# Two heads at a time in three attention branches: probability-times-value products that alternate between partitions of a PSUM bank

## The chip, the cores and the metric

One core of one Trainium2 chip runs the whole program. The metric is device time in microseconds (us) of one execution, given as the median of several runs. Engines are named as in the profile: PE is TensorE's matmul row, PEld its weight load row, DVE is VectorE, ACT is ScalarE, POOL is GpSimd, SP is SyncE, whose queue issues nearly all DMAs. L634 is line 634 of the kernel.

## The reference, cut to what matters

Two transformer layers over 512 tokens of width 1024. Each has a mixer of four attention branches and then a feed-forward part (dense in layer 0, 8 experts in layer 1). All products keep float32 accuracy. What the change touches is the softmax attention of branches b, c and d:

```python
# b: 4 heads, 96-wide queries and keys, 64-wide values, causal, blocks of 128 queries
s = einsum('bqhd,bkhd->bhqk', qf[:, i*128:L], kf[:, :L]) * scale        # L = 128 * (i + 1)
p = softmax(where(mask, s, -inf), axis=-1)
outs.append(einsum('bhqk,bkhd->bqhd', p, v[:, :L]))
# c: 8 query heads on 2 key heads, 32-wide, a band of two blocks of 128 keys, bias, a sink in the denominator
# d: 3 patterns of 4 heads, 32-wide, bands of strided keys, mixed by their log-sum-exp
```

## The kernel before

**The stage.** In each layer `merge` interleaves generators: `attend`, which runs the units of branches b, d and c in that order, and a filler chain of `front_c` (projections for branch c) and `gates` (gated output products of branches a, b and d, the `mm` matmuls of L208, L210 and L212). The framework's scheduler then orders each engine's instructions when the program is built, by program order and by when it expects operands and buffers to be ready; on the chip each engine runs its list in that fixed order.

**Units.** `attend` (L614) takes units from `branch_b`, `branch_d` and `branch_c`. A unit is part of one head: the scores of one or two blocks of 128 queries (PE into an `sc` bank), `smax` (L596: DVE adds mask or bias, takes the maximum, writes to a `big` tile) and `expo` (L603: ACT). In branch b a head has three units (query blocks 0 and 1 together, block 2, block 3, that is 3, 3 and 4 blocks of 128 keys), in branches c and d two (3 and 4 blocks, in d's second group 4 and 4). That makes 12, 16 and 16 units in a layer: 20 with 3 blocks and 24 with 4.

**Lags.** `step` (L639) keeps three units in the list `ts` and up to three in `vs` (`lt=3`, `lv=3`). For each new unit it first calls `times` for the oldest turned unit, then `turn` for the oldest unit in `ts`. `turn` (L618) transposes the unit's 3 or 4 probability blocks on PE (L622) into a `tr` bank and copies that bank to a `pt` tile, on ACT (L628) and DVE (L626) in turn. `times` (L632) multiplies: for each block one float32 matmul (L634) with the value block, 128x32 (c, d) or 128x64 (b), as the stationary operand and the 128x128 transposed probabilities as the moving one. A float32 matmul shows in the trace as two passes, each a weight load and a matmul record. The output goes to 32 or 64 partitions of one `pv` bank, the partitions of that head: `rs`, or `slice(64 * s_, 64 * s_ + 64)`. The last unit of a bank calls `after`, which scales and evacuates it.

**Heads.** `heads(h)` prepares the operands of one head ahead of its units. In branch b it is two `head_T` calls (L730: 8 transposes, then `split` into `op` tiles, ACT L187 and DVE L188), called for the next head after the third query block's scores. In branches c and d it is `stack`: DMAs on the SP queue (L844) into `op` or, for odd heads, `opx` tiles, and in d a bias table from `toeplitz` (L332); each head calls it for the next one as its first unit begins. Branch c asks for its bias table (`fsw`) as the head begins. `op` has 10 buffers, `opx` 8, `big` 5, `pt` 3, `sc` 2, `tr` 2, `pv` 1, the bias tables `fb` 2.

Of the kernel before, what the change touches and what calls it, by code (L numbers as in the profile page):

```python
# [7 lines left out]
F32 = mybir.dt.float32  # L8
# [29 lines left out]
B_ = dict(mm=3, sc=2, tr=2, pv=1, t2=11, op=10, big=5, u96=2, pt=3, small=24, go=6, raw=4, whi=3, wlo=2, fb=2, gx=4, mraw=4, mhi=5, mlo=5, mg=3, r4=8)  # L38
# [54 lines left out]
def build(tc, A, out, dbg=None):  # L93
# [5 lines left out]
    with es:  # L99
# [249 lines left out]
        def mixer(l, norm, follow, fargs):  # L349
# [264 lines left out]
            def attend(units):  # L614

                def turn(p, perm, blocks, mid, after):  # L618
                    got = mid and mid()
                    ps = trp()  # L620
                    for b, (c, *_) in enumerate(blocks):
                        nc.tensor.transpose(ps[:, 128 * b:128 * b + 128], p[:, c:c + 128], perm)  # L622
                    pt = at.tile([128, 512], F32, tag="pt", name="pt", bufs=B_["pt"])
                    n = 128 * len(blocks)
                    if attend.n % 2:
                        nc.vector.tensor_copy(pt[:, :n], ps[:, :n])  # L626
                    else:
# [20 lines left out]
                for u in units:  # L648
# [5 lines left out]
                    yield  # L654
                while ts or vs:
                    step(True)
                    yield
# [112 lines left out]
            def branch_b(qt, kt, v):  # L770
# [5 lines left out]
                if True:  # L776
                    nxt = heads(0)
                    for h in range(4):
                        t, s_ = divmod(h, 2)
                        if s_ == 0:  # L780
                            pv, nm, li = Bank(), stat(2), stat(2)
                        qh, ql, kh, kl = nxt
                        p = big(1280)
                        c = 0
                        blocks = []
                        for i in range(NB):
                            w = 128 * (i + 1)
                            if i != 1:
                                bank = sc()
                            ps = bank[:, 128:384] if i == 1 else bank[:, :w]  # L790
                            qs = slice(128 * i, 128 * i + 128)
                            scores3(ps, qh[:, qs], ql[:, qs], kh[:, :w], kl[:, :w])
                            smax(ps, causal[:, 512 - w:], p[:, c:c + w], BIG, nm[:, i, s_:s_ + 1])
                            expo(p[:, c:c + w], nm[:, i, s_:s_ + 1], li[:, i, s_:s_ + 1])
                            for kb in range(i + 1):
                                blocks.append((c + 128 * kb, pv, (slice(64 * s_, 64 * s_ + 64), qs),
                                               v[:, kb, 64 * h:64 * h + 64], kb == 0, kb == i))
                            c += w
                            if i == 2 and h < 3:
                                nxt = heads(h + 1)  # L800
                            if i:
# [11 lines left out]
                                yield p, ident, blocks, mid, after  # L813
                                blocks = []
# [50 lines left out]
            def branch_c(kn, q, v):  # L865
# [4 lines left out]
                nxt = heads(0)  # L870
                yield iter(())
                o = []

                if True:
                    for h in range(8):
                        t, s_ = divmod(h, 4)
                        rs = slice(32 * s_, 32 * s_ + 32)
                        if s_ == 0:
                            pv, nm, li = Bank(), stat(4), stat(4)
                            kst = nxt[0]  # L880
                        qst = nxt[1]
# [4 lines left out]
                        p = big(896)  # L886
                        c = 0
                        for i in range(NB):
                            nb = 2 if i else 1
                            w = 128 * nb  # L890
                            k0 = 128 * (i + 1) - w
                            qs = slice(128 * i, 128 * i + 128)
                            if i % 2 == 0:
                                bank = sc()
                                b0 = c
                                blocks = []
                            ps = bank[:, c - b0:c - b0 + w]
                            nc.tensor.matmul(ps, qst[:, qs], kst[:, k0:k0 + w], start=True, stop=True)
                            smax(ps, f[:, 256 - w:], p[:, c:c + w], nsink[:, h:h + 1], nm[:, i, s_:s_ + 1])
                            expo(p[:, c:c + w], nm[:, i, s_:s_ + 1], li[:, i, s_:s_ + 1])  # L900
                            for b in range(nb):
                                blocks.append((c + 128 * b, pv, (rs, qs), v[:, k0 // 128 + b, 32 * t:32 * t + 32],
                                               b == 0, b == nb - 1))
                            c += w
                            if i % 2:
                                mid = after = None
                                if s_ == 3 and i == NB - 1:
                                    nc.vector.tensor_sub(nm, nm, nsink[:, 4 * t:4 * t + 4].unsqueeze(1)
                                                         .to_broadcast([128, NB, 4]))
                                    nc.scalar.activation(nm, nm, AF.Exp)  # L910
                                    nc.vector.tensor_add(li, li, nm)
                                    nc.vector.reciprocal(li, li)

                                    def mid(rb=widen(li)):
                                        return spread(rb, flip)

                                    def after(r, t=t, pv=pv):
                                        o.append(oevac(pv[:], r, t2() if t else None))
                                        if t:
                                            st["oc"] = o  # L920
                                yield p, flip, blocks, mid, after
# [15 lines left out]
            def branch_d(q, k, v):  # L937
# [13 lines left out]
                nxt = heads(0, 0)  # L951
# [51 lines left out]
                for g in range(2):  # L1003
                    for h in range(4):
                        rs = slice(32 * h, 32 * h + 32)
                        qst, kst, f = nxt
# [3 lines left out]
                        c = 0  # L1010
                        for b0 in (0, 2):
                            ps = sc()
                            blocks = []
                            c0 = c
                            cols = []
                            for b in (b0, b0 + 1):
                                bs = slice(128 * b, 128 * b + 128)
                                if g:
                                    w = 256
                                    for j in range(2):  # L1020
                                        nc.tensor.matmul(ps[:, c - c0 + 128 * j:c - c0 + 128 * j + 128],
                                                         qst[j][:, bs], kst[j][:, bs], start=True, stop=True)
                                        blocks.append((c + 128 * j, pv[1], (rs, bs),
                                                       v[:, b, 128 + 128 * j + 32 * h:160 + 128 * j + 32 * h],
                                                       j == 0, j == 1))
                                else:
                                    w = 256 if b else 128
                                    k0 = 128 * b + 128 - w
                                    nc.tensor.matmul(ps[:, c - c0:c - c0 + w], qst[0][:, bs], kst[0][:, k0:k0 + w],
                                                     start=True, stop=True)  # L1030
                                    for j in range(w // 128):
# [863 lines left out]
```

## Time and profile before

| | |
|---|---|
| median of 3 runs | 1424.32 us (1423.17 to 1425.55) |
| the profiled execution | 1422.78 us, span 1420.8 us |
| granted clock over the span | 0.986 |
| PE busy | 1360.3 us, 96% |
| DVE, ACT, POOL busy | 841.8 us, 777.9 us, 383.9 us |

The span is the time from the first to the last instruction of the program. A busy time is the union of an engine's records. Matmuls are pipelined, so their records overlap, and a busy PE is not necessarily one at its peak. The chain that ended last is followed back from the last instruction, at each step to what released it.

### The profile page before, as it was taken

How to read it: one execution, taken by the hardware profiler on the slowest of the kernel's cores; microseconds unless marked ns; L12 is line 12 of the kernel's file. 1: busy time of each engine (PE TensorE's matmuls, PEld its weight loads, DVE VectorE, ACT ScalarE, POOL GpSimd, SP SyncE). 2: the span in 40 equal slices, each digit the busy share in tenths (PEclk: the TensorE clock that was granted, in tenths of full speed). 3: DMA queues.
4: the chain of work that ended last, by engine and by line, in shares of the span. 5: the costliest groups of instructions: out<-in, count | busy, mean ns of one | idle time of the engine just before them, and what ended most of it. 6: DMA issues, size and time to landing. Idle time of an engine off the chain costs nothing.

```text
span 1420.8 us, 21146 instructions
## 1 busy us (share of the span) xinstructions
PE 1360.3 (96%) x7826; PEld 1108.8 (78%) x7826; DVE 841.8 (59%) x1488; ACT 777.9 (55%) x1492; POOL 383.9 (27%) x307
## 2 busy tenths in 40 slices
PE   7999999999999999999999999999998899999996
PEld 5777667877778888888777767787685788989995
DVE  5344656666664444433433655656564879988883
ACT  5255666666453222233234566666544767778884
POOL 2000110023031112101000120002302577877764
PEclk9999999999999999999999999999999899999998
DMA  9422325551373333344432332554453588999994
GB/s 260 111 66 72 105 82 174 156 166 58 93 222 89 95 99 93 108 148 141 116 86 60 95 95 95 184 155 144 137 162 102 196 269 248 305 302 311 315 304 97
DMA packets 241116, 217.15 MB, mean 153 GB/s; under 512 B 12408, under 2 KB 212080, under 8 KB 241008
## 3 DMA queue, kind: packets, MB, share of 16 engines
q1 hardware_dynamic: 237352, 206.25, 47.8%
q0 software_dynamic: 3456, 9.44, 3.1%
q8 instruction: 63, 1.03, 0.3%
q14 instruction: 45, 0.37, 0.1%
q10 hardware_dynamic: 200, 0.06, 0.0%
HBM read 187.32 MB, written 28.38 MB: 152 GB/s over the span
## 4 chain that ended last, share of the span: by engine, by line
PE 74%; issue 10%; ACT 5%; DVE 4%; POOL 4%; DMA 3%; POOLq 0%; SPq 0%; another core or an unknown queue 0%; ACTq 0%; DVEq 0%
PE mm L210 13%; PE mm L212 12%; PE mm L208 11%; PE mg L1586 8%; PE pv L634 5%; PE mg L1589 4%; PE tr L622 3%; PE sc L1119 1%; PE tr L1119 1%; PE pv L576 1%; PE sc L530 1%; POOL mlo L1354 1%; PE tr L822 1%; DVE mlo L1354 1%; PE mg L1434 1%
## 5 line engine op out<-in xcount | busy, mean ns | idle before, releaser
L200 ACT CAST whi<-raw 128x1024 fp32r<-128x1024 f32 (+1 forms) x144 | 141.9, 986 | 190.9 <-PE mm L210 93.6
L1354 DVE TENSOR_TENSOR mlo<-mraw,mhi 128x768 bf16<-128x768 f32 (+2 forms) x160 | 181.3, 1141 | 26.8 <-ACT mhi L1351 25.8
L201 DVE TENSOR_TENSOR wlo<-raw,whi 128x1024 fp32r<-128x1024 f32 (+1 forms) x144 | 165.7, 1153 | 45.4 <-PE mm L212 25.6
L208 PE MATMUL mm<-xh,whi 128*128 128x512 f32 x608 | 162.7, 397 | 2.8 <-ACT xh L190 2.8
L210 PE MATMUL mm<-xl,whi 128*128 128x512 f32 x608 | 155.3, 395 | 0.0
L1351 ACT CAST mhi<-mraw 128x1024 fp32r<-128x1024 f32 (+1 forms) x160 | 151.9, 963 | 4.8 <-DMA mraw<-in_w_down_exp_dram 3.5
L212 PE MATMUL mm<-xh,wlo 128*128 128x512 f32 x608 | 151.1, 390 | 0.0
L1586 PE MATMUL mg<-xcat,mhi 128*128 128x320 f32 x768 | 137.8, 322 | 1.0 <-DVE xcat L188 1.0
L210 PEld LDWEIGHTS mm<-xl,whi 128*128 128x128 f32 x608 | 114.1, 189 | 26.1 <-issue 2.9
L212 PEld LDWEIGHTS mm<-xh,wlo 128*128 128x128 f32 x608 | 114.3, 188 | 24.1 <-issue 0.3
L208 PEld LDWEIGHTS mm<-xh,whi 128*128 128x128 f32 x608 | 110.4, 188 | 23.7 <-ACT xh L190 3.6
L1586 PEld LDWEIGHTS mg<-xcat,mhi 128*128 128x128 f32 x768 | 114.9, 191 | 1.5 <-DVE xcat L188 0.7
L502 POOL TENSOR_TENSOR y<-y,t 128x512 f32<-128x512 f32 x32 | 42.1, 1320 | 258.0 <-DVE t L501 256.4
L1354 POOL TENSOR_TENSOR mlo<-mraw,mhi 128x256 bf16<-128x256 f32 x80 | 97.1, 1216 | 29.9 <-ACT mhi L1351 12.7
L1589 PEld LDWEIGHTS <-mlo 128*128 128x128 bf16 x1152 | 77.3, 99 | 18.0 <-DVE mlo L1354 0.8
L387 DVE TENSOR_TENSOR t<-mm,rb 128x512 f32<-128x512 f32 x41 | 28.3, 691 | 90.9 <-PE mm L212 88.6
L634 PE MATMUL pv<-pt,v 128*32 128x128 f32 (+1 forms) x624 | 81.7, 279 | 0.1
L1586 PE MATMUL mg<-acat,mhi 128*128 128x320 f32 x384 | 75.6, 330 | 2.6 <-POOL acat L1631 2.6
L1184 POOL TENSOR_TENSOR t<-t,t 128x512 f32<-128x512 f32 x16 | 34.2, 2138 | 143.6 <-DVE t L1183 143.6
L247 POOL TENSOR_TENSOR t<-t,t 128x512 f32<-128x512 f32 x21 | 32.8, 1561 | 148.7 <-ACT t L246 148.4
L634 PEld LDWEIGHTS pv<-pt,v 128*32 128x32 f32 (+1 forms) x624 | 60.0, 117 | 15.3 <-issue 9.5
L1589 PE MATMUL mg<-xb,mlo 128*128 128x160 bf16 x768 | 70.5, 235 | 0.4 <-DVE mlo L1354 0.4
(368 smaller groups left out, 2712.5 us busy)
## 6 DMA issues: line engine op xcount, KB each, us to landing
mraw<-in_w_gu_exp_dram SPq DMA_DIRECT2D x48, 1024.0 KB, 7.9
mraw<-in_w_down_exp_dram SPq DMA_DIRECT2D x32, 768.0 KB, 5.3
raw<-in_w_in_dram SPq DMA_DIRECT2D x46, 512.0 KB, 3.9
raw<-in_w_gu_dense_dram SPq DMA_DIRECT2D x32, 512.0 KB, 4.1
heads<-t SPq DMA_DIRECT2D x36, 256.0 KB, 2.0
opx<-heads SPq DMA_DIRECT2D x68, 128.0 KB, 3.4
op<-heads SPq DMA_DIRECT2D x68, 128.0 KB, 3.2
raw<-in_w_down_dense_dram SPq DMA_DIRECT2D x16, 512.0 KB, 4.1
```

What stands on the lines that cost most here:

```text
L200: (nc.gpsimd.tensor_copy if pool else nc.scalar.copy)(hi, raw)
L201: (eng or nc.vector).tensor_sub(lo, raw, hi.bitcast(F32))
L208: nc.tensor.matmul(ps, wh[:, k, :], xs[k][0], start=first and k == 0, stop=False)
L210: nc.tensor.matmul(ps, wh[:, k, :], xs[k][1], start=False, stop=False)
L212: nc.tensor.matmul(ps, wl[:, k, :], xs[k][0], start=False, stop=last and k == n - 1)
L502: (nc.vector if br in YV else nc.gpsimd).tensor_add(y[m], y[m], u)
L622: nc.tensor.transpose(ps[:, 128 * b:128 * b + 128], p[:, c:c + 128], perm)
L634: nc.tensor.matmul(pv[i], lt, pt[:, 128 * b:128 * b + 128], start=st, stop=sp_)
L1351: nc.scalar.copy(self.hi[:, a:b], self.raw[:, a:b])
L1354: eng.tensor_sub(self.lo[:, a:b], self.raw[:, a:b], self.hi[:, a:b].bitcast(F32))
L1586: nc.tensor.matmul(ps[:, j, :2 * CAP], wh[:, k, :], cat[:, k, :], start=k == 0, stop=False, skip_group_check=True)
L1589: nc.tensor.matmul(ps[:, j, :CAP], wl[:, k, :], xb[:, k, :], start=False, stop=k == kk - 1, skip_group_check=True)
```

## The change

`step` takes two turned units at a time and `times` runs their products alternately, block by block. So that the two units of a pair belong to two heads, each branch now makes its units in the order of head pairs: unit 1 of heads h and h+1, then unit 2 of both. Operands of two heads are prepared together: in branch b those of heads 2 and 3 after the last scores of heads 0 and 1, in branches c and d those of the next pair as a pair begins. The bias tables have 4 buffers of 128x256 instead of 2 padded to 128x512. Arithmetic, matmuls and their shapes, lags `lt` and `lv` and the other buffer numbers stay.

```diff
-B_ = dict(..., fb=2, ...)
+B_ = dict(..., fb=4, ...)
...
-                def times(pt, blocks, after, got):
-                    for b, (c, pv, i, lt, st, sp_) in enumerate(blocks):
-                        nc.tensor.matmul(pv[i], lt, pt[:, 128 * b:128 * b + 128], start=st, stop=sp_)
-                    if after:
-                        after(got)
+                def times(*pair):
+                    for b in range(len(pair[0][1])):
+                        for pt, blocks, *_ in pair:
+                            c, pv, i, lt, st, sp_ = blocks[b]
+                            nc.tensor.matmul(pv[i], lt, pt[:, 128 * b:128 * b + 128], start=st, stop=sp_)
+                    for _, _, after, got in pair:
+                        if after:
+                            after(got)
...
-                    if len(vs) >= (1 if last else P_["lv"]):
-                        times(*vs.pop(0))
+                    if len(vs) >= (2 if last else P_["lv"]):
+                        times(vs.pop(0), vs.pop(0))
                     if len(ts) >= (1 if last else P_["lt"] + 1):
                         vs.append(turn(*ts.pop(0)))
...
# branch_b
-                    nxt = heads(0)
-                    for h in range(4):
-                        t, s_ = divmod(h, 2)
...
+                nxt = [heads(0), heads(1)]
+                for t in range(2):
+                    pv, nm, li = Bank(), stat(2), stat(2)
+                    cur, nxt = nxt, []
+                    ps_, banks, c, blocks = [big(1280), big(1280)], [None] * 2, [0, 0], [[], []]
+                    for i in range(NB):
+                        for s_ in range(2):
+                            h = 2 * t + s_
+                            qh, ql, kh, kl = cur[s_]
...
-                            if i == 2 and h < 3:
-                                nxt = heads(h + 1)
+                            if i == NB - 1 and t == 0:
+                                nxt.append(heads(2 + s_))
...
# branch_c
-                    for h in range(8):
...
-                        if h < 7:
-                            nxt = heads(h + 1)
-                        f = at.tile([128, 256], F32, tag="fb", name="fsw", bufs=B_["fb"], padded_shape=[128, 512])
-                        toeplitz(f, h, 256, 256)
+                for hp in range(0, 8, 2):
...
+                    if hp < 6:
+                        nxt = [heads(hp + 2), heads(hp + 3)]
+                    f, p, c = [], [], [0, 0]
+                    for j in range(2):
+                        f.append(at.tile([128, 256], F32, tag="fb", name="fsw", bufs=B_["fb"]))
+                        toeplitz(f[j], hp + j, 256, 256)
+                        p.append(big(896))
+                    for i0 in (0, 2):
+                        for j in range(2):
+                            h, s_ = hp + j, s0 + j
...
# branch_d
-                nxt = heads(0, 0)
+                nxt = [heads(0, 0), heads(0, 1)]
...
-                    for h in range(4):
...
-                        if (g, h) != (1, 3):
-                            nxt = heads(*divmod(4 * g + h + 1, 4))
-                        p = big(1024)
+                    for hp in (0, 2):
+                        cur = nxt
+                        if (g, hp) != (1, 2):
+                            nxt = [heads(*divmod(4 * g + hp + j, 4)) for j in (2, 3)]
+                        p, c = [big(1024), big(1024)], [0, 0]
                         for b0 in (0, 2):
+                            for a_ in range(2):
+                                h = hp + a_
```

## Rows read from the trace of the kernel before

**Rows 1.** The page's first section: busy time of each engine, share, instructions

```profile
PE 1360.3 (96%) x7826; PEld 1108.8 (78%) x7826; DVE 841.8 (59%) x1488; ACT 777.9 (55%) x1492; POOL 383.9 (27%) x307
```

**Rows 2.** Busy time by stretch, all instructions (columns: the second line)

```profile
core 0: us, PE busy (x) PEld busy (x) DVE busy (x) ACT busy (x) POOL busy (x), PEclk, DMA share, GB/s
225.00:352.00 127.00, 123.95 (x798) 98.67 (x798) 81.08 (x240) 80.12 (x223) 20.54 (x16) 1.00 0.48 142
891.00:1019.00 128.00, 125.02 (x788) 99.28 (x788) 80.18 (x239) 79.63 (x222) 19.71 (x16) 0.97 0.50 145
1075.00:1420.00 345.00, 317.63 (x2717) 287.47 (x2715) 269.48 (x388) 245.42 (x414) 235.44 (x194) 0.96 0.82 248
312.00:340.00 28.00, 25.75 (x177) 20.56 (x176) 19.39 (x61) 18.23 (x57) 8.69 (x7) 1.00 0.40 119
...
225.00:245.00 20.00, 19.85 (x118) 15.30 (x118) 14.12 (x33) 15.31 (x34) 0.00 (x0) 1.00 0.69 220
```

**Rows 3.** Busy time by stretch, L634 alone: length, PE (records), PEld, clock, DMA

```profile
225.00:352.00 127.00, 40.44 (x312) 29.79 (x312) 1.00 0.48 142
891.00:1019.00 128.00, 41.30 (x312) 30.25 (x312) 0.97 0.50 145
```

**Rows 4.** PE's timeline in branch c: start, us, engine, line, operation, records

```profile
310.63 0.40 PE L212 MATMUL mm<-goh,wlo 128*128 128x512 f32 x1
310.95 1.06 PE L634 MATMUL pv<-pt,v 128*32 128x128 f32 x8
311.94 0.55 PE L622 MATMUL tr<-c_flip,big 128*128 128x128 f32 x3
...
315.66 0.62 PE L212 MATMUL mm<-goh,wlo 128*128 128x512 f32 x2
...
323.22 0.84 PE L634 MATMUL pv<-pt,v 128*32 128x128 f32 x6
...
324.89 1.31 PE L634 MATMUL pv<-pt,v 128*32 128x128 f32 x14
...
331.21 0.39 PE L898 MATMUL sc<-opx,op 128*128 128x256 f32 x1 [1.39 <-DVE stat L596]
...
338.10 1.96 PE L634 MATMUL pv<-pt,v 128*32 128x128 f32 x20
```

**Rows 5.** The tile view of pv: duration min/median/max ns, first and last start

```profile
L634 PEld LDWEIGHTS pv<-pt,v x624: 106/110/177, 225.9 to 1018.2; 128*32 128x32 f32 x116, 128*64 128x64 f32 x40
L634 PE MATMUL pv<-pt,v x624: 272/273/423, 225.9 to 1018.3; 128*32 128x128 f32 x116, 128*64 128x128 f32 x40
```

**Rows 6.** PE's timeline at four instants: the L634 records then running

```profile
321.94 0.38 PE L634 MATMUL pv<-pt,v 128*32 128x128 f32 x2
...
325.35 0.41 PE L634 MATMUL pv<-pt,v 128*32 128x128 f32 x4
...
338.67 0.49 PE L634 MATMUL pv<-pt,v 128*32 128x128 f32 x3
...
339.22 0.52 PE L634 MATMUL pv<-pt,v 128*32 128x128 f32 x5
```

**Rows 7.** Timelines of ACT, DVE and SP in branch b

```profile
232.05 1.05 ACT L187 CAST op<-tr 96x512 fp32r<-96x512 f32 x2
...
237.28 0.48 ACT L628 COPY pt<-tr 128x384 f32<-128x384 f32 x1
...
233.94 1.28 DVE L188 TENSOR_TENSOR op<-tr,op 96x512 fp32r<-96x512 f32 x2
...
238.93 0.68 DVE L626 COPY pt<-tr 128x512 f32<-128x512 f32 x1
...
233.98 10.14 SPq L844 DMA_DIRECT2D op<-heads  x16
```

**Rows 8.** Waits from 225 to 352 us: total, times, longest

```profile
ACT pt L628 <- PE tr L622: 16.5, 10, 2.6
...
DVE big L596 <- DMA fsw<-relvec: 3.8, 3, 1.7
```

More of the change, by code (lines that the diff above doesn't have):

```diff
@@ L35 @@
 NFT = DFE // 128
-B_ = dict(mm=3, sc=2, tr=2, pv=1, t2=11, op=10, big=5, u96=2, pt=3, small=24, go=6, raw=4, whi=3, wlo=2, fb=2, gx=4, mraw=4, mhi=5, mlo=5, mg=3, r4=8)
+B_ = dict(mm=3, sc=2, tr=2, pv=1, t2=11, op=10, big=5, u96=2, pt=3, small=24, go=6, raw=4, whi=3, wlo=2, fb=4, gx=4, mraw=4, mhi=5, mlo=5, mg=3, r4=8)
 P_ = dict(d=0.0, c=0.0, g=0.0, h=0.0, fb=0.0, fd=0.3, na=54, pa=0, lt=3, lv=3, hg=0, hb=0, ho=0, sa=15, fa=0.125, pb=0, pc=0.4, pd=0.15, eg=0, eb=0)
@@ L654, in attend @@
                     yield
+                assert not len(ts) + len(vs) & 1
                 while ts or vs:
@@ L774, in heads @@
                     return head_T(qt, h) + head_T(kt, h)
-                if True:
-                    nxt = heads(0)
-                    for h in range(4):
-                        t, s_ = divmod(h, 2)
[L780 to L786, printed above, removed]
+                nxt = [heads(0), heads(1)]
@@ L787, in branch_b @@
+                for t in range(2):
[6 more added lines that the diff above has]
+                            qh, ql, kh, kl = cur[s_]
+                            p = ps_[s_]
                             w = 128 * (i + 1)
@@ L798, in branch_b @@
-                            c += w
-                            if i == 2 and h < 3:
-                                nxt = heads(h + 1)
+                                blocks[s_].append((c[s_] + 128 * kb, pv, (slice(64 * s_, 64 * s_ + 64), qs),
+                                                   v[:, kb, 64 * h:64 * h + 64], kb == 0, kb == i))
+                            c[s_] += w
+                            if i == NB - 1 and t == 0:
+                                nxt.append(heads(2 + s_))
@@ L812, in after @@
                                             st["ob"] = o
-                                yield p, ident, blocks, mid, after
-                                blocks = []
+                                yield p, ident, blocks[s_], mid, after
+                                blocks[s_] = []
             def headnorm(t, gain, rev, streams=False):
@@ L868, in heads @@
                     return None if s_ else stack(kn, 32 * t, 1, t % 2), stack(q[t], 32 * s_, 0, s_ % 2)
-                nxt = heads(0)
+                nxt = [heads(0), heads(1)]
                 yield iter(())
                 o = []
-                if True:
-                    for h in range(8):
[L876 to L881, printed above, removed]
-                        if h < 7:
-                            nxt = heads(h + 1)
-                        f = at.tile([128, 256], F32, tag="fb", name="fsw", bufs=B_["fb"], padded_shape=[128, 512])
-                        toeplitz(f, h, 256, 256)
[L886 to L921, printed above, removed]
@@ new lines, in branch_c, with mid, after @@
+                for hp in range(0, 8, 2):
+                    t, s0 = divmod(hp, 4)
+                    if s0 == 0:
+                        pv, nm, li = Bank(), stat(4), stat(4)
+                        kst = nxt[0][0]
+                    cur = nxt
[9 more added lines that the diff above has]
+                            h, s_ = hp + j, s0 + j
+                            rs = slice(32 * s_, 32 * s_ + 32)
+                            bank = sc()
+                            b0 = c[j]
+                            blocks = []
+                            for i in (i0, i0 + 1):
+                                nb = 2 if i else 1
+                                w = 128 * nb
+                                k0 = 128 * (i + 1) - w
+                                qs = slice(128 * i, 128 * i + 128)
+                                ps = bank[:, c[j] - b0:c[j] - b0 + w]
+                                pc = p[j][:, c[j]:c[j] + w]
+                                nc.tensor.matmul(ps, cur[j][1][:, qs], kst[:, k0:k0 + w], start=True, stop=True)
+                                smax(ps, f[j][:, 256 - w:], pc, nsink[:, h:h + 1], nm[:, i, s_:s_ + 1])
+                                expo(pc, nm[:, i, s_:s_ + 1], li[:, i, s_:s_ + 1])
+                                for b in range(nb):
+                                    blocks.append((c[j] + 128 * b, pv, (rs, qs), v[:, k0 // 128 + b, 32 * t:32 * t + 32],
+                                                   b == 0, b == nb - 1))
+                                c[j] += w
+                            mid = after = None
+                            if s_ == 3 and i0:
+                                nc.vector.tensor_sub(nm, nm, nsink[:, 4 * t:4 * t + 4].unsqueeze(1)
+                                                     .to_broadcast([128, NB, 4]))
+                                nc.scalar.activation(nm, nm, AF.Exp)
+                                nc.vector.tensor_add(li, li, nm)
+                                nc.vector.reciprocal(li, li)
+                                def mid(rb=widen(li)):
+                                    return spread(rb, flip)
+                                def after(r, t=t, pv=pv):
+                                    o.append(oevac(pv[:], r, t2() if t else None))
+                                    if t:
+                                        st["oc"] = o
+                            yield p[j], flip, blocks, mid, after
@@ L1003, in branch_d @@
                 for g in range(2):
-                    for h in range(4):
-                        rs = slice(32 * h, 32 * h + 32)
-                        qst, kst, f = nxt
-                        if (g, h) != (1, 3):
-                            nxt = heads(*divmod(4 * g + h + 1, 4))
-                        p = big(1024)
-                        c = 0
-                        for b0 in (0, 2):
[L1012 to L1031, printed above, removed]
-                                        blocks.append((c + 128 * j, pv[0], (rs, bs),
-                                                       v[:, k0 // 128 + j, 32 * h:32 * h + 32],
-                                                       j == 0, j == w // 128 - 1))
-                                cols.append((b, c, w))
-                                c += w
-                            for b, c1, w in cols:
-                                nm = ml[g][:, b, 0, h:h + 1]
-                                smax(ps[:, c1 - c0:c1 - c0 + w], f[:, 256 - w:], p[:, c1:c1 + w], BIG, nm)
-                                expo(p[:, c1:c1 + w], nm, ml[g][:, b, 1, h:h + 1])
-                            yield p, flip, blocks, None, (keep, combine)[g] if (h, b0) == (3, 2) else None
@@ new lines, in branch_d @@
+                    for hp in (0, 2):
+                        cur = nxt
+                        if (g, hp) != (1, 2):
+                            nxt = [heads(*divmod(4 * g + hp + j, 4)) for j in (2, 3)]
+                        p, c = [big(1024), big(1024)], [0, 0]
+                        for b0 in (0, 2):
+                            for a_ in range(2):
+                                h = hp + a_
+                                rs = slice(32 * h, 32 * h + 32)
+                                qst, kst, f = cur[a_]
+                                ps = sc()
+                                blocks = []
+                                c0 = c[a_]
+                                cols = []
+                                for b in (b0, b0 + 1):
+                                    bs = slice(128 * b, 128 * b + 128)
+                                    c1 = c[a_]
+                                    if g:
+                                        w = 256
+                                        for j in range(2):
+                                            nc.tensor.matmul(ps[:, c1 - c0 + 128 * j:c1 - c0 + 128 * j + 128],
+                                                             qst[j][:, bs], kst[j][:, bs], start=True, stop=True)
+                                            blocks.append((c1 + 128 * j, pv[1], (rs, bs),
+                                                           v[:, b, 128 + 128 * j + 32 * h:160 + 128 * j + 32 * h],
+                                                           j == 0, j == 1))
+                                    else:
+                                        w = 256 if b else 128
+                                        k0 = 128 * b + 128 - w
+                                        nc.tensor.matmul(ps[:, c1 - c0:c1 - c0 + w], qst[0][:, bs], kst[0][:, k0:k0 + w],
+                                                         start=True, stop=True)
+                                        for j in range(w // 128):
+                                            blocks.append((c1 + 128 * j, pv[0], (rs, bs),
+                                                           v[:, k0 // 128 + j, 32 * h:32 * h + 32],
+                                                           j == 0, j == w // 128 - 1))
+                                    cols.append((b, c1, w))
+                                    c[a_] += w
+                                for b, c1, w in cols:
+                                    nm = ml[g][:, b, 0, h:h + 1]
+                                    smax(ps[:, c1 - c0:c1 - c0 + w], f[:, 256 - w:], p[a_][:, c1:c1 + w], BIG, nm)
+                                    expo(p[a_][:, c1:c1 + w], nm, ml[g][:, b, 1, h:h + 1])
+                                yield p[a_], flip, blocks, None, (keep, combine)[g] if (h, b0) == (3, 2) else None
```

11 lines of the change are left out of this document (5 added, 6 removed).

## The prediction

> **What bounds the kernel now.** I began with the page's busy times: PE is busy for 96% of the span and DVE and ACT for little over half of theirs [rows 1]. That is an average, so I asked for the two stretches in which the pairs can act, from the first L634 record to the last of each layer: 225 to 352 us and 891 to 1019 us. There PE is busy 123.95 of 127 us and 125.02 of 128 us, DVE about 63%, ACT about 63% [rows 2]. The reader is to see that PE leaves 3 us in each stretch, so that time taken out of PE is time taken out of the kernel until another engine or a wait shows. The products of L634 hold 40.44 and 41.30 us of PE there, 81.74 us in all, a third of the stage [rows 3].
>
> **What one burst costs now.** A unit's `times` is a run of 6 or 8 passes. In PE's timeline 8 passes take 1.06 us and 6 take 0.84 us [rows 4], so a pass adds (1.06 - 0.84) / 2 = 0.11 us, though its record lasts 0.273 us [rows 5]: passes of one head follow each other at 0.11 us, two to three of them in flight (2 at 321.94, 3 at 338.67 [rows 6]).
>
> A burst also costs something at both ends. The 512-column matmuls before one follow each other at 0.62 - 0.39 = 0.23 us, so the one that starts at 310.63 frees the array's input at 310.86; the burst starts at 310.95, 0.09 later. Its last pass starts at 310.95 + 1.06 - 0.27 = 311.74 and the transposes start at 311.94, 0.20 later, 0.09 more than a pass's pace [rows 4]. That is 0.18 us a burst.
>
> **Whether two heads overlap.** The trace of before has a few places where the scheduler put a burst of one head straight behind one of the next head. The run of 14 at 324.89 is 8 passes of one head and 6 of the next, on other partitions. One after the other they would take 1.06 + 6 x 0.11 = 1.72 us; they take 1.31 [rows 4]. In its overlapping part 4 records are in flight, where a single head has 2 or 3 [rows 6]. The run of 20 at 338.10 is the control: it begins with 14 passes of one head, and 0.57 us into it only 3 records are in flight; when the next head's 6 follow, there are 5 [rows 6]. It takes 1.96 us, where 20 passes in a row would take 1.06 + 12 x 0.11 = 2.38 [rows 4]. So the second head rides along, as far as PE's order lets it start early: 0.4 us of its 0.66 us are saved when it stands behind, and with alternating blocks it can start behind the first two passes.
>
> The Trainium skill, in "TensorE: Matmul & The Clock Gate", section "Part 3: Packing small matmuls — row/col tiling", says that weight loads overlap with running matmuls "only when row_grp differs"; all these products use all 128 rows. By that rule every pass of the second head would wait with its load, and pairs would give nothing but fewer bursts (a rival below). The 14 loads of the run above last 0.106 us or more each [rows 5], 1.48 us together, within a run of 1.31 us that has their matmuls in it too, so here the trace does not agree.
>
> **The change part by part.**
>
> *Alternating products.* 88 units become 44 pairs: 20 of 3 blocks a head and 24 of 4. If the second head is hidden but for one half of a pass (between 0, all hidden, and 0.11, a whole pass behind; I take 0.05), a pair takes 0.89 or 1.11 us: 20 x 0.89 + 24 x 1.11 = 44.4 us in place of 81.74 us [rows 3]. That is -37.3 us (bounds -36 and -38.5). The nearest rows, 0.4 us saved in a pair that does not alternate, would give 44 x 0.4 = -17.6 us; I take the alternating value, because the control shows that it is the order alone that delays the second head.
>
> *Fewer bursts.* PE's timeline has 41 runs of L634 in each stretch, 82; there will be 44. 38 x 0.18 = -6.8 us.
>
> So PE loses 44.1 us of work, 22 us in each layer.
>
> *Operands of two heads at a time, branch b.* Of 10 `op` buffers heads 0 and 1 hold 8, so the 8 tiles of heads 2 and 3 can only be written after the last scores of heads 0 and 1, where before the next head was prepared one unit ahead. A head is 4 transposes twice, two casts on ACT (0.525 us each) and two subtractions on DVE (0.64 us each) [rows 7]. Cover: the filler's `mm` products and the six units still in the lags. If that cover is gone, both heads' casts and subtractions lie open, 2 x (1.05 + 1.28) = 4.7 us a layer; below it is 0. I take 1.5 us a layer: +3 us.
>
> *Operands of two heads, branches c and d.* The same DMAs, twice as many at a time, a pair ahead instead of a head ahead, which is the same share of lead and twice as long in time. The SP queue issued 16 of these from 233.98 to 244.12, before any unit of branch d [rows 7], so the fetches run far ahead of use. Behind them on SP stand the gates' weights and bias tables. 0.
>
> *Four bias buffers.* Same bytes. A table of branch c can be fetched while two pairs are in hand, not two heads. DVE waited 3.8 us for tables in the first stretch [rows 8], and PE once sat 1.39 us behind that wait [rows 4]. Between 0 and -1.4 us a layer; I count 0.
>
> *Lag of the second unit.* `vs` now empties by two, so one unit of a pair has two steps between its copy and its product in place of three. A step is 127 / 44 = 2.9 us now, a copy takes 0.48 to 0.68 us [rows 7], and it is the copies that wait for the transposes, 16.5 us on ACT [rows 8], rather than PE for copies. With steps of 2.4 us two of them are 4.8 us: 0.
>
> *Heads interleaved.* The same number of scores, reductions, exponentials and copies; two `big` tiles a pair, with the units in the lag four of the five in use. 0.
>
> **What the stage gives back.** PE's busy time falls to 123.95 - 22.05 = 101.9 us and 125.02 - 22.05 = 103.0 us. DVE's 81 and ACT's 80 us stay. PE idles 2.4% of the stretch now. Where DVE and ACT are loaded at 69% and 65% (312 to 340 us) or 78% and 71% (1075 to 1420 us) it idles 8% [rows 2]; after the change they stand at about 75%. Part of the idle time in 312 to 340 is the table wait that now has more lead. I take 6%, between the two: 101.9 / 0.94 = 108.4 and 103.0 / 0.94 = 109.5 us, that is -18.6 and -18.5, together -37 us. The 3 us of branch b's handover are a part of this idle time, not added to it. What follows the stretches starts as they end, so the span moves by as much: 1420.8 - 37 = 1383.8 us, the profiled execution from 1422.78 to 1385.8 us, and the median, 1.5 us above it, from 1424.32 to 1387 us.
>
> **The rivals.**
>
> *The cover runs out.* The products overlap, but PE then waits for ACT and DVE. For it: in the first 20 us ACT is busy 15.31 us [rows 2], and with some 2.5 us less of PE that is 87% of the stretch; that is where branch b's handover comes as well. Against it: over the whole stage ACT needs only 80 us of some 108. With PE idle 12% a stretch lasts 101.9 / 0.88 = 116 us, so about -11 us each: -22; with 15% it is -14. 1401 to 1411 us.
>
> *No overlap in alternation.* PE might run alternating passes one after another; then the change does not do what it says and only the bursts' ends go: -6.8 us, 1417.5 us. Against it stand the runs of 14 and 20; for it, that no run in this trace alternates. The rule on weight loads cited above would end here too.
>
> *Slower: the second unit's `pt` is late.* PE's order is fixed at build, so a product that waits for its copy holds everything behind it: the next transposes, scores and the filler. Were each of the 44 pairs to wait, the gain is gone at 44.1 / 44 = 1.0 us a pair, and above 1.07 us the kernel is slower by over 0.2%; at 1.5 us it is +22, 1446 us. Against it: two steps of lead against a copy of 0.7 us. For it: one step of three is gone, and ACT, which makes half of the copies, is the fuller engine in branch b.
>
> **How the numbers follow.** The forecast has 0.70; cover running out 0.14; no overlap 0.06; late `pt` 0.06; and 0.04 for these together ending within 0.2% (2.8 us, about what a measurement of this kernel can tell from no change). The forecast's own range: PE idle 8% gives -32 us, with the whole 9.4 us of handover open -23, 1401 us; PE idle 2.4% with the table waits gone gives -45 - 3 = -48, 1376 us. A little over that for a gain in the fetches: 1374. Upward the range reaches over the second case to 1410 us; what is left out is the cases behind it and the tails, less than 2 in 10. Faster 0.90, same 0.04, slower 0.06.
>
> **What the profile after would show.** The stage's L634 busy time near 44 us, not 82, in runs of 12 and 16 records that last about 0.9 and 1.1 us, 22 a layer, with four or five records in flight. Stretches of about 109 us with PE busy near 94%. Runs of 16 that last 1.9 us would prove the second rival; idle time of PE released by the copies of L626 or L628 right before L634 the third; gaps before the scores of L590 in the middle of branch b the handover; PE busy below 88% with ACT as releaser the first. The prediction is wrong if PE's saving is there but the stretches do not shorten with it, or if the scheduler splits the pairs.

## The result, and the profile after

The changed kernel takes 1386.78 us in the median (1386.01 to 1389.95, 4 runs) against 1424.61 us: ratio 0.974, 95% interval 0.9722 to 0.9757. Forecast were 1387 us, in a range of 1374 to 1410.

Busy time by stretch, from the first to the last product record of each layer; first all instructions, then the products alone (now L637), as in [rows 2, 3]:

```profile
core 0: us, PE busy (x) PEld busy (x) DVE busy (x) ACT busy (x) POOL busy (x), PEclk, DMA share, GB/s
225.60:333.20 107.60, 104.99 (x782) 83.58 (x780) 77.88 (x237) 79.35 (x221) 18.36 (x15) 0.98 0.54 161
877.70:985.30 107.60, 105.00 (x781) 83.56 (x780) 77.90 (x237) 79.27 (x221) 18.36 (x15) 0.98 0.55 161
...
225.60:333.20 107.60, 24.34 (x312) 16.78 (x312) 0.98 0.54 161
877.70:985.30 107.60, 24.35 (x312) 16.77 (x312) 0.98 0.55 161
```

The stage shrank from 124.4 and 127.4 us, cut in the same way, to 107.6 in both layers: -36.6 us. The products hold 48.69 us in these windows, 49.12 us with their last records whole, in place of 81.74. DVE and ACT have nearly as much work as before, and PE is again busy for 97.6% of the stage: it is still what bounds it.

PE's timeline in branches b and d, product lines, then the two longest waits of PE in the stage (columns as in [rows 4]):

```profile
254.74 1.09 PE L637 MATMUL pv<-pt,v 128*64 128x128 f32 x16
...
259.21 0.85 PE L637 MATMUL pv<-pt,v 128*32 128x128 f32 x12
...
263.58 1.07 PE L637 MATMUL pv<-pt,v 128*32 128x128 f32 x16
...
276.49 0.30 PE L905 MATMUL sc<-op,opx 128*128 128x128 f32 x1 [0.40 <-issue]
277.98 0.73 PE L208 MATMUL mm<-goh,whi 128*128 128x512 f32 x2 [1.18 <-ACT goh L187]
```

Sixteen passes of two heads take 1.07 us in branch d (1.09 in branch b), as long as eight of one head did (1.06), and twelve 0.85, as long as six did (0.84) [rows 4]. The scheduler took some pairs apart, here in branch b:

```profile
225.64 0.43 PE L637 MATMUL pv<-pt,v 128*64 128x128 f32 x2
...
228.02 0.66 PE L637 MATMUL pv<-pt,v 128*64 128x128 f32 x8
...
229.18 0.43 PE L637 MATMUL pv<-pt,v 128*64 128x128 f32 x2
...
233.23 0.87 PE L637 MATMUL pv<-pt,v 128*64 128x128 f32 x10
```

Twelve passes of one pair stand in runs of 2, 8 and 2. Over both layers there are 60 runs, where 82 were and 44 were forecast: of the eight more in a layer four are in branch b's six pairs and four in the sixteen pairs of branches d and c.

The profiled execution is the slowest of the four (1389.95 us, span 1388.1, 32.7 us less than before); what it lacks of 36.6 us lies outside the stages. Stretches with the same work show a lower mean granted clock in this execution: first the kernel before, then the changed one.

```profile
411.00:446.00 35.00, 31.48 (x129) 24.65 (x129) 18.73 (x20) 13.89 (x18) 9.42 (x7) 0.95 0.37 107
730.00:775.00 45.00, 44.00 (x208) 33.51 (x208) 17.77 (x26) 21.54 (x46) 2.88 (x2) 1.00 0.26 68
```

```profile
395.00:430.00 35.00, 31.49 (x123) 24.47 (x122) 17.41 (x18) 13.87 (x18) 8.88 (x6) 0.90 0.37 107
715.00:760.00 45.00, 44.01 (x201) 33.65 (x199) 17.77 (x26) 20.82 (x44) 2.88 (x2) 0.96 0.25 68
```

### The profile page after: what moved, and what is told of

The parts are those of the page before. It is cut to its first block, busy times and chain, and to the rows that moved or that the text cites. A ratio compares the mean times of both kernels' runs of the same rounds, so it can differ in the third digit from the quotient of the medians.

```text
span 1388.1 us, 21150 instructions
## 1 busy us (share of the span) xinstructions
PE 1329.2 (96%) x7826; PEld 1084.6 (78%) x7826; DVE 837.4 (60%) x1488; ACT 778.9 (56%) x1492; POOL 387.4 (28%) x307
## 4 chain that ended last, share of the span: by engine, by line
PE 74%; issue 11%; ACT 5%; POOL 4%; DVE 3%; DMA 2%; POOLq 0%; another core or an unknown queue 0%; SPq 0%; ACTq 0%; DVEq 0%
PE mm L210 13%; PE mm L212 13%; PE mm L208 12%; PE mg L1595 9%; PE mg L1598 4%; PE pv L637 3%; PE tr L623 3%; PE sc L1128 1%; PE tr L1128 1%; PE pv L576 1%; POOL mlo L1363 1%; PE sc L530 1%; PE tr L827 1%; PE mg L1443 1%; DVE mlo L1363 1%
## 5 line engine op out<-in xcount | busy, mean ns | idle before, releaser
L1363 POOL TENSOR_TENSOR mlo<-mraw,mhi 128x256 bf16<-128x256 f32 x80 | 100.2, 1256 | 28.8 <-ACT mhi L1360 23.3
L387 DVE TENSOR_TENSOR t<-mm,rb 128x512 f32<-128x512 f32 x41 | 28.3, 690 | 83.4 <-PE mm L212 81.1
L208 PE MATMUL mm<-goh,whi 128*128 128x512 f32 x176 | 66.9, 425 | 6.0 <-ACT goh L187 6.0
L1187 DVE TENSOR_TENSOR t<-mm,rb 128x512 f32<-128x512 f32 x32 | 22.1, 692 | 72.9 <-PE mm L212 72.9
```

The costliest lines, as they stand in the source:

```text
L208: nc.tensor.matmul(ps, wh[:, k, :], xs[k][0], start=first and k == 0, stop=False)
L1363: eng.tensor_sub(self.lo[:, a:b], self.raw[:, a:b], self.hi[:, a:b].bitcast(F32))
```

## The experiments

All runs in one table. "Stage" is the time from the first product record's start to the last one's in each layer, "products" their busy time, "runs" how often PE starts on them.

| kernel | median us | ratio to before (95%) | stage us | products us | runs |
|---|---|---|---|---|---|
| before | 1424.61 | | 124.2, 127.3 | 81.7 | 82 |
| changed | 1386.78 | 0.974 (0.9722 to 0.9757) | 107.5, 107.5 | 49.1 | 60 |
| e1, one head after the other | 1401.32 | 0.9853 (0.9815 to 0.9891) | 113.7, 113.7 | 65.0 | 58 |
| e2, single products | 1418.61 | 0.9963 (0.9948 to 0.9979) | 123.9, 123.9 | 82.4 | 90 |
| e3, two units of a head | 1412.35 | 0.9921 (0.9894 to 0.9947) | 119.5, 119.4 | 77.5 | 56 |
| e4, four bias buffers | 1417.85 | 0.9966 (0.995 to 0.9982) | 122.7, 122.7 | 82.1 | 84 |
| e5, lag 4 | 1382.59 | 0.9718 (0.9701 to 0.9736) | 103.7, 104.0 | 47.5 | 56 |
| e6, four heads in c and d | 1399.12 | 0.983 (0.9814 to 0.9846) | 112.5, 110.1 | 37.2 | 52 |
| e7, four heads in c, lag 4 | 1391.01 | 0.9778 (0.9746 to 0.9811) | 107.1, 107.3 | 41.6 | 52 |
| e8, e6 with the reload elsewhere | 1397.97 | 0.9817 (0.9791 to 0.9843) | 109.4, 109.5 | 37.2 | 50 |
| e9, lag 5 | 1379.91 | 0.9699 (0.9668 to 0.973) | 103.2, 103.0 | 47.5 | 56 |
| changed, again | 1386.81 | 0.9741 (0.9711 to 0.9771) | 106.0, 106.0 | 49.1 | 60 |
| e10, lag 4 again | 1382.37 | 0.9703 (0.9682 to 0.9724) | 103.7, 104.7 | 47.5 | 56 |
| e11, lag 5 again | 1379.63 | 0.9695 (0.9676 to 0.9715) | 102.9, 102.7 | 47.5 | 56 |

Each ratio is to the kernel before on the same chip: e1 to e4 ran on one chip, e5 and e6 on one, e7, e8, e9 and the changed kernel again on one, e10 and e11 on one.

**e1: is it the alternation?**

```diff
-                    for b in range(len(pair[0][1])):
-                        for pt, blocks, *_ in pair:
+                    for pt, blocks, *_ in pair:
+                        for b in range(len(blocks)):
```

> The changed kernel, but within a pair all products of the first head come before all products of the second. If the gain is two heads' products running at once (my theory), the second head can start only when the first has few passes left, as in the run of 14 of the kernel before: a pair of 16 passes takes about 1.5 us instead of 1.07 and one of 12 about 1.1 instead of 0.84, so 24 x 0.45 + 20 x 0.25 = 16 us are lost: about 1402 us (1397 to 1407). If the gain is that there are half as many runs of products, or the new order of heads, nothing changes: 1387 us (1385 to 1389).

```profile
261.12 1.09 PE L637 MATMUL pv<-pt,v 128*32 128x128 f32 x12
265.77 1.53 PE L637 MATMUL pv<-pt,v 128*32 128x128 f32 x16
```

PE's timeline of e1: 1.53 and 1.09 us in place of 1.07 and 0.85, and 14.5 us more in the median, as the theory had it. At the same clock of 1.00 a stage takes 113.7 us, the changed kernel's 106.0 (its second execution), and the products, 7.9 us longer, account for all of it. The order of the blocks alone is worth that.

**e2: the new order of heads without pairs of products.**

```diff
-                    if len(vs) >= (2 if last else P_["lv"]):
-                        times(vs.pop(0), vs.pop(0))
+                    if len(vs) >= (1 if last else P_["lv"]):
+                        times(vs.pop(0))
```

> The changed kernel with its order of heads, its double preparation of operands and its four bias buffers, but with the products of one unit at a time, as before. My theory: without two heads in one run nothing overlaps but what happens to stand together; L634's products hold about 80 us again: 1415 to 1425 us. Rival, the order of heads and the longer lead of operands and tables give the gain: under 1400 us.

```profile
268.78 0.84 PE L637 MATMUL pv<-pt,v 128*32 128x128 f32 x6
...
270.43 1.06 PE L637 MATMUL pv<-pt,v 128*32 128x128 f32 x8
```

PE's timeline of e2: 8 passes take 1.06 us again and 6 take 0.84. The products hold 82.4 us, so hardly any overlap is left, and the kernel is as fast as e4, which shares its four bias buffers and nothing else. Order of heads and double preparation of operands are worth nothing that can be measured by themselves.

**e3: fewer runs without other partitions**, on the kernel before. In b pairs can cross from one head to the next; in c and d both units are of one head.

```diff
-                def times(pt, blocks, after, got):
+                def times(*pair):
+                    for pt, blocks, *_ in pair:
...
-                    if len(vs) >= (1 if last else P_["lv"]):
-                        times(*vs.pop(0))
+                    if len(vs) >= (2 if last else P_["lv"]):
+                        times(vs.pop(0), vs.pop(0))
```

> The kernel before with its order of heads, but products of two units in a row come together, the first's before the second's; in branches c and d both are of the same head and the same partitions. It has the fewer runs of products without the overlap. My theory: 38 runs fewer by 0.18 us, 6.8 us less: about 1417 us (1412 to 1421). Rival, what costs is the change between products and other matmuls and not the products: under 1400 us.

```profile
279.11 1.72 PE L635 MATMUL pv<-pt,v 128*32 128x128 f32 x14
284.65 1.93 PE L635 MATMUL pv<-pt,v 128*32 128x128 f32 x16
```

In e3's timeline sixteen passes of one head take 1.93 us: on the same partitions no second product rides along and a pass still adds 0.11 us, however close the passes stand. The gain of 10.75 us lies at the edge of the expected range. It is not overlap: in a layer of e3 only two runs overlap, pairs of branch b that cross heads (14 passes in 1.36 us), and in the kernel before four did. The products fell by 4.2 us (81.7 to 77.5) all the same, because a joined run of 16 takes 1.93 us and two runs of 8 take 2 x 1.06 = 2.12: 26 runs fewer are some 26 x 0.19 = 4.9 us. I had left that out. The ends of the runs are the rest: in the first layer, at a clock of 1.00 in both, PE's other busy time fell by 2.1 us, 13 runs by 0.16. The second layer also ran at a mean clock of 1.00, where the trace of before has 0.97.

**e4: the bias buffers alone**, on the kernel before.

```diff
-B_ = dict(..., fb=2, ...)
+B_ = dict(..., fb=4, ...)
...
-                        f = at.tile([128, 256], F32, tag="fb", name="fsw", bufs=B_["fb"], padded_shape=[128, 512])
+                        f = at.tile([128, 256], F32, tag="fb", name="fsw", bufs=B_["fb"])
```

> The kernel before with four bias buffers of 128x256 instead of two padded to 128x512, and nothing else. My theory: 0 to 2.8 us less, 1422 to 1425 us. Rival, the waits for tables held the stage: 1415 us or less.

More than the 2.8 us that I had at most, and less than the rival: 4.8 us by the ratio. The stages lost 1.5 and 4.5 us. Busy time by stretch in branch c of layer 1, the kernel before and then e4:

```profile
985.00:1004.00 19.00, 16.86 (x94) 13.33 (x94) 10.14 (x35) 11.06 (x36) 1.35 (x2) 0.82 0.24 58
```

```profile
985.00:1004.00 19.00, 18.13 (x127) 14.58 (x126) 13.24 (x45) 13.46 (x42) 5.03 (x4) 1.00 0.18 56
```

PE's timeline of the kernel before, inside the stretch:

```profile
996.51 0.58 PE L898 MATMUL sc<-opx,op 128*128 128x256 f32 x1 [1.28 <-DVE stat L596]
997.02 1.92 PE L634 MATMUL pv<-pt,v 128*32 128x128 f32 x8
```

Before, PE waited there for a table, and behind the wait eight passes take 1.92 us and the stretch's mean granted clock is 0.82, part of it at the lower of its two levels; in e4 the wait is gone and the clock is 1.00. The same wait in the first layer (1.39 us [rows 4]) had no fall behind it: the clock was 1.00, and there e4 gains the 1.5 us. So the wait was priced about right; the other 3 us, the clock's, are seen in one layer of one execution, and that the wait brought them is not shown.

**e5, e9, e10, e11: one and two more steps of lag**, on the changed kernel (in e9 and e11 the copy buffers share their space with tiles of the projection stage).

```diff
-pt=3, ... lv=3
+pt=4, ... lv=4        # e5, e10
+pt=5, ... lv=5        # e9, e11
...
-            gm = at.tile([128, 2, 96], F32, name="gm")
+            gm = t2(w=192).rearrange("p (a b) -> p a b", a=2)
```

> The changed kernel with one more step between a unit's copy and its products (lag 4 and 4 copy buffers instead of 3 and 3; to make room the 768 bytes of a gain row move to another pool). The trace of the changed kernel has 60 runs of products instead of 44: some pairs are split, and products hold 48.7 us instead of 44.4. If they are split because the second unit's copy comes late in the order made at build, the runs fall to about 46 and the products to about 44 us, some 6 us of PE: 1381 us (1378 to 1385). If the split has another cause, or PE is no longer what bounds the stage: 1385 to 1389 us.

> Pairs as in the changed kernel, with lag 5 and 5 copy buffers (one step more than the run with lag 4). If late copies still split pairs, the 56 runs of products of lag 4 fall further and the time to about 1379 us; if what is left of the splits has another cause, 1381 to 1385 us.

> The run with one more step of lag again, beside the one with two more on one chip, five rounds: a ratio to the kernel before of 0.9705 to 0.972, under that of the changed kernel (0.974).

> The run with two more steps of lag again. If the second step gives something, a ratio 0.001 or more below that of the run beside it; if all that matters came with the first step, the same within 0.001.

The first step gives some 4 us in both runs (by the ratios 0.22 and 0.38%, with intervals that overlap that of the changed kernel). e5 landed in my range and e10 just under it, but not for my reason: the runs fell only to 56 and the products to 47.5 us, so late copies explain few of the splits. With lag 5 the runs stay at 56, so e9's 1379.91 us, the forecast for fewer runs, has another cause too. Busy time by stretch of e5:

```profile
225.60:329.20 103.60, 102.29 (x780) 81.94 (x780) 77.55 (x237) 79.32 (x221) 18.38 (x15) 1.00 0.57 169
871.30:975.40 104.10, 102.92 (x781) 81.87 (x780) 77.45 (x237) 79.47 (x221) 18.52 (x15) 1.00 0.58 167
```

Against the second execution of the changed kernel (106.0 us, also at a clock of 1.00) a stage has 2.0 to 2.3 us less: 0.8 of products, 0.4 of run ends, and PE's idle time falls from 2.6 to 1.2 or 1.3 us; the wait of 1.18 us for `goh` above is gone. Lag 5 beside lag 4 has a ratio 0.0008 lower, by my measure the same, with intervals that overlap widely; the traces have its stages 0.5 to 1.9 us shorter. Whether the second step gives anything stays open. Both are faster than the kernel before and, with lag 5, the interval of e11 (0.9676 to 0.9715) lies under that of the changed kernel's first measurement.

**e6, e7, e8: four heads.**

```diff
-                nxt = [heads(0, 0), heads(0, 1)]
+                nxt = [heads(0, j) for j in range(4)]
...
-                    if len(vs) >= (2 if last else P_["lv"]):
-                        times(vs.pop(0), vs.pop(0))
+                    if vs and len(vs) >= vs[0][4] + (not last):
+                        times(*[vs.pop(0) for _ in range(vs[0][4])])
...
# e8
-                        nc.sync.dma_start(t, od)
+                        nc.gpsimd.dma_start(t, od)
```

> The changed kernel with four heads at a time in branches c and d, whose heads use 32 partitions each; branch b keeps pairs. Copy buffers 5 (they share their space with tiles of the projection stage), operands of four heads prepared together. My theory, that products of different partitions run at once, goes on to four: 16 pairs in each layer become 8 runs of four heads at about the time of one pair, 8.7 us of PE less in each layer: 1369 us if PE idles as little as now, 1377 us if it idles 6% of the stage. Rival, only two can run at once: 1385 to 1388 us. Rival, ACT and DVE now bound the stage: 1378 to 1386 us, with PE idle over 10% of it.

> The run with one more step of lag, with four heads at a time in branch c alone; branches b and d in pairs. In c a head needs one fresh 128x512 operand tile, in d up to four, so the operand buffers suffice. If products of four heads go on to overlap and PE bounds the stage: 8 pairs in each layer become 4 runs of four, 4.3 us of PE less a layer, 1374 us (1370 to 1378). If the end of branch c is held by its reductions on DVE instead: 1380 to 1385 us.

> The run with four heads in c and d, with one line changed: the gates' reload of a branch's output goes out on GpSimd's DMA queue and not on SP's. In the trace of that run PE waits from 274 to 282 us for such a reload, which stood on SP behind eleven transfers of head operands. If that queue is the loss, the stage of 112 us falls to about 104 and the kernel to 1385 us (1380 to 1390). If the number of operand buffers is the loss, nothing much changes: 1395 to 1400 us.

PE's timeline of e6: a run of four heads, then three of its waits.

```profile
271.49 1.08 PE L637 MATMUL pv<-pt,v 128*32 128x128 f32 x32
...
277.60 0.30 PE L907 MATMUL sc<-op,opx 128*128 128x128 f32 x1 [0.43 <-DMA opx<-heads]
279.19 1.21 PE L975 MATMUL tr<-mq,c_every 128*128 128x32 f32 x8 [1.29 <-DVE mq L970]
...
282.61 1.22 PE L208 MATMUL mm<-goh,whi 128*128 128x512 f32 x2 [0.81 <-ACT goh L187]
```

Thirty-two passes take 1.08 us: four heads overlap as two do. But in a layer only two of the eight groups came out whole, one run of 24 passes and this one of 32; the scheduler took the others apart, and the products fell by some 12 us, to 37.2. All the same the kernel is 12 us slower than with pairs, outside every range that I gave, and e7 missed both of its ranges too. The stretch views say why in part, e6 first, then e8, then e7:

```profile
226.30:338.90 112.60, 105.45 (x782) 81.21 (x780) 77.90 (x237) 79.69 (x221) 18.00 (x15) 0.94 0.51 154
```

```profile
226.30:335.80 109.50, 101.26 (x781) 79.56 (x780) 78.00 (x237) 79.67 (x221) 19.61 (x18) 0.97 0.55 158
```

```profile
226.40:333.70 107.30, 103.10 (x781) 80.50 (x780) 77.25 (x237) 78.92 (x221) 18.00 (x15) 0.98 0.54 161
```

PE idles 7.2, 8.2 and 4.2 us of the stage where the pairs leave 2.6, and the mean clock is 0.94, 0.97 and 0.98. The rival that ACT and DVE bound the stage wanted PE idle for over 10% of it; it is 4 to 8%. In e6 the chain goes through the gates' reload, issued behind the operands of four heads:

```profile
275.67 1.24 SPq L850 DMA_DIRECT2D opx<-heads  x2
277.01 1.00 SPq L476 DMA_DIRECT2D t<-o  x2
```

My theory that SP's queue is the loss fell with e8: with the reload on GpSimd's queue the first stage is 3 us shorter, but the kernel is the same within the intervals, and PE now waits 3.9 us for `goh` in one piece. I had read e6 too harshly: from 274 to 282.6 us PE is busy for 5.64 of 8.60 us, and only 0.81 us of its idle time stand right before the reload's use. Four heads in c alone (e7, lag 4) are better than in c and d (e6), and still slower than the pairs of e5 with the same lag; e7 changes the lag and the operands at once, so which of the two helped is not shown. Which of operands, reloads and reductions would have to move for four heads to pay stays open.

**The changed kernel again.**

> The changed kernel again, beside the three others on one chip: 1385 to 1389 us. It tells whether the half-rate stretches of PE's clock at about 279, 405, 733 and 931 us in its first trace come back in another execution; in the stage I expect them again, since they follow a wait of PE that the order of instructions sets, and not those at 733 us.

The median came back within 0.03 us. The stage's mean clock was 1.00 this time, so there my expectation missed: PE's idle times of 0.40 and 1.18 us at about 277 and 278 us were in both executions, the lower clock behind them (0.81 from 275 to 284 us in the first) only in one. The stretch at 733 us did not come back, as I had said; the one near 405 did (0.86 from 400 to 412 us).

## Why the prediction was right, point by point

- *PE bounds the stage, two heads' products overlap.* Right, and shown: 16 passes take 1.07 us alternating, 1.53 one head after the other (e1), 1.93 on the same partitions (e3). The Trainium skill says in "TensorE: Matmul & The Clock Gate", section "Part 3: Packing small matmuls — row/col tiling", that weight loads overlap with running matmuls only where the rows of the array differ. All these products use all 128 rows, and the trace does not agree: here other output partitions are enough (16 passes in 1.07 us).
- *The price of a pair, 0.89 and 1.11 us.* 0.85 and 1.07: the second head is hidden entirely, so the half pass was one too many. The bounds of its sum were also added up too narrow: 0 to 0.11 us a pair give -39.5 to -34.7 us, not -38.5 to -36.
- *44 pairs, products -37.3, run ends -6.8, PE -44.1 us.* The step that was mis-sized: 60 runs, since the scheduler splits pairs, which the prediction itself had named as a sign of being wrong. The products fell by 32.6 us and the run ends by some 22 x 0.18 = 4.0, so PE lost about 37 us; its busy time in the stages fell by 35.8 us in the profiled execution and by 38.7 in the second, which ran them at a clock of 1.00.
- *PE will idle 6%.* Also mis-sized: 2.4%, as before, though ACT is now busy for 74% of the stage and DVE for 72%, near the 75% from which I had taken the 6%. The two errors cancel, and -37 us came out as -36.6 in the stages. That the median came within 0.3 us of the forecast is luck; the mechanism and the direction are not.
- *Branch b's handover, up to 4.7 us a layer.* Not there: PE is busy 19.22 of the first 19.4 us of the stage.
- *Operands of two heads in c and d: 0.* Right (e2 beside e4).
- *Four bias buffers: 0, at most 1.4 us a layer.* Too small: 4.8 us in all (e4). In the layer where the clock is the same it was 1.5 us; the rest stands where the clock of the kernel before had fallen behind the wait in its second layer, and its cause stays open.
- *The lag of the second unit: 0.* PE's waits in the stage name no copy, as said, yet one more step gives some 4 us (e5): with it there are fewer split pairs and a wait that stands elsewhere is gone. That the lag works through the order that the scheduler makes is my reading, not shown. It did not come near the rival's 44 us.

By ratios the whole of -2.6% divides so: bias buffers 0.34% (e4), order of heads nothing (e2, 0.37% with them), products in pairs but not alternating 1.1% (e1 from e2), alternation another 1.1% (from e1). The third part holds the fewer runs and the overlap of pairs that stand one behind the other; these runs do not part the two.

## What to carry to other kernels

Products that fill only 32 or 64 of the output partitions can run at once when their neighbours in PE's order write other partitions; look in the trace for an accidental neighbour before building it, and alternate block by block, since the order decides how much of it is had. Look in the trace also at whether the pairs come out of the scheduler whole. More heads need not pay more: two paid 2.6%, four in branches c and d 1.7%, with less time in products but more idle time and a lower clock of PE, and why stays open. After such a change look again at lags that were set for single units.

## What the runs showed of the hardware

- Float32 products that alternate between four sets of 32 output partitions, 32 passes, take 1.08 us (e6) where 8 passes on one set take 1.06; on two sets of 64 partitions 16 passes take 1.09 us.
- A pass for the next set of partitions that stands behind eight for another starts early but not at once: 16 passes take 1.53 us, not 1.07 and not 1.93. In e1's trace two passes begin within 0.01 us of each other first at the fifth pass of eight, and at the third of six.
- Behind short waits of PE the granted clock sometimes falls and sometimes does not: in the kernel before it was 0.82 over 19 us around a wait of 1.28 us in the second layer and 1.00 around one of 1.39 us in the first; in the changed kernel 0.81 and 1.00 behind the same waits in two executions.
